# A batched matmul whose engine programs are written by hand, with one counter for every hand-over

## The chip, the cores and the metric

The kernel runs on one core of a Trainium2 chip. The metric is the device time in microseconds (us) from launch to end; before the change the median of 11 runs is 262.08 us (261.91 to 262.48). The profile shows one execution in detail, with the time of each instruction, of each wait and of the DMA traffic.

The engines that matter here are TensorE (PE; its weight loads appear as PEld), VectorE (DVE), ScalarE (ACT) and SyncE (SP). SP does no arithmetic: it issues the transfers between HBM and the on-chip memory. They all go through one queue, which is served by 16 DMA engines.

## The reference

```
x: (16, 768, 512) float32      # batch, k, m
y: (16, 768, 1024) float32     # batch, k, n
out = np.einsum('bkm,bkn->bmn', x, y).astype(np.float32)   # (16, 512, 1024)
```

For each of 16 batches, the product of the transposed x with y. A batch reads 1.57 MB of x and 3.15 MB of y, and writes 2.10 MB.

## The kernel before

A batch is the unit of work. k is split as 128 partitions times KT = 6 slices, m as 128 rows times MT = 4 (`mo`), and n as NT = 2 halves of 512. The stages of a batch are:

1. SP loads x of the batch into a float32 staging tile `xs` (L59) and y into `ys` (L62). There are two buffers of each. The last batch loads y in two halves of three k slices each.
2. VectorE casts `xs` to the bf16 tile `x_sb` in one instruction (L67) and `ys` to `y_sb` in two halves (L70).
3. TensorE runs 48 matmuls of 128x128 by 128x512 (L83): for each of the four `mo`, two halves of n, six k slices added up in PSUM. The last batch does this in two passes, one for each half of k, so that it can start on the first half of y.
4. ScalarE copies each finished `mo` (128x1024, two PSUM banks) into the output tile `o_sb` (L88), four copies for a batch.
5. SP stores `o_sb` (L52). The store of batch b-4 is issued after the loads of batch b; after the loop the last four stores follow. There are five output tiles, and four PSUM buffers of two banks each.

The order of the instructions on each engine is the order in which the program issues them; the tile framework inserts the semaphore waits. On SP this order is: x0 y0, x1 y1, x2 y2, x3 y3, x4 y4 store0, x5 y5 store1, and so on. SP waits in front of a transfer until it may be issued, and everything behind it on SP waits too. The load of x of batch b into its staging buffer waits until the cast of x of batch b-2 has read the buffer; the load of y of batch b waits for both casts of y of batch b-2. Nothing else holds the loads back.

Of the kernel before, what the change touches and what calls it, by code (L numbers as in the profile page):

```python
# [1 line left out]

_os.environ.setdefault("NEURON_RT_ULTRASERVER_MODE", "4")

# [1 line left out]

# [4 lines left out]


@with_exitstack
def kernel(
    ctx: ExitStack,
    tc: tile.TileContext,
    x: bass.AP,
    y: bass.AP,
    out: bass.AP,
):  # L20
    nc = tc.nc
    P = 128
    FP32 = mybir.dt.float32
    BF16 = mybir.dt.bfloat16

    B, K, M = x.shape
    _, _, N = y.shape
    KT = K // P
    MT = M // P
    NF = 512  # L30
    NT = N // NF

    x_v = x.rearrange("b (p ko) m -> b p ko m", ko=KT)
    y_v = y.rearrange("b (p ko) n -> b p ko n", ko=KT)
    o_v = out.rearrange("b (p mo) n -> b p mo n", mo=MT)

    xs_pool = ctx.enter_context(tc.tile_pool(name="xs_pool", bufs=2))
    ys_pool = ctx.enter_context(tc.tile_pool(name="ys_pool", bufs=2))  # L40
    x_pool = ctx.enter_context(tc.tile_pool(name="x_pool", bufs=2))
    y_pool = ctx.enter_context(tc.tile_pool(name="y_pool", bufs=2))
    o_pool = ctx.enter_context(tc.tile_pool(name="o_pool", bufs=5))
    psum = ctx.enter_context(tc.tile_pool(name="psum", bufs=4, space=bass.MemoryType.PSUM))
    LAG = 4
    KH = KT // 2
    o_tiles = {}

    def store(b):
        o_sb = o_tiles.pop(b)  # L50

        nc.sync.dma_start(o_v[b], o_sb[:])  # L52

    with tc.manual_schedule():
        for b in range(B):
            xs = xs_pool.tile([P, KT, M], FP32, name="xs")
            ys = ys_pool.tile([P, KT, N], FP32, name="ys")
            halves = 2 if b == B - 1 else 1
            nc.sync.dma_start(xs[:], x_v[b])  # L59
            for h in range(halves):  # L60
                ks = slice(h * KT // halves, (h + 1) * KT // halves)
                nc.sync.dma_start(ys[:, ks], y_v[b, :, ks])  # L62
            if b >= LAG:
                store(b - LAG)
            x_sb = x_pool.tile([P, KT, M], BF16, name="x_sb")
            y_sb = y_pool.tile([P, KT, N], BF16, name="y_sb")
            nc.vector.tensor_copy(x_sb[:], xs[:])  # L67
            for h in range(2):
                ks = slice(h * KH, (h + 1) * KH)
                nc.vector.tensor_copy(y_sb[:, ks], ys[:, ks])  # L70
            x_w = x_sb[:].rearrange("p k (j mo) -> p k mo j", mo=MT)
            o_sb = o_pool.tile([P, MT, N], FP32, name="o_sb")
            o_tiles[b] = o_sb
            ps = {}


            for h in range(halves):
                for mo in range(MT):
                    if h == 0:
                        ps[mo] = psum.tile([P, NT, NF], FP32, name="ps")  # L80
                    for nt in range(NT):
                        for kt in range(h * KT // halves, (h + 1) * KT // halves):
                            nc.tensor.matmul(  # L83
                                ps[mo][:, nt], x_w[:, kt, mo],
                                y_sb[:, kt, nt * NF:(nt + 1) * NF],
                                start=(kt == 0), stop=(kt == KT - 1))
                    if h == halves - 1:
                        nc.scalar.copy(o_sb[:, mo].rearrange("p (t f) -> p t f", f=NF), ps[mo][:])  # L88
        for b in sorted(o_tiles):
            store(b)  # L90


# [1 line left out]
_INS = ['x', 'y']  # L94
_OUTS = [((16, 512, 1024), 'float32')]


# [23 lines left out]
```

## Time and profile before

| | |
|---|---|
| median of 11 runs | 262.08 us |
| the profiled execution: time, span | 262.1 us, 260.3 us |
| PE busy | 187.5 us, 72% (753 matmuls recorded) |
| DVE busy | 83.1 us, 32% |
| ACT busy | 66.2 us, 25% |
| DMA traffic | 109.18 MB, mean 419 GB/s |
| HBM read, written | 75.50 MB, 33.55 MB |

The span runs from the first to the last instruction; 1.8 us of the profiled execution's time lie outside it. Times inside the profile are counted from the start of the span.

### The profile page before, as it was taken

What the parts mean: (1) busy time and instruction counts of PE and PEld (TensorE: products, weight loads), DVE (VectorE), ACT (ScalarE), POOL (GpSimd) and SP (SyncE); (2) the same over time, 40 slices, a digit from 0 to 9 for tenths busy, and PEclk for the clock granted to TensorE, in tenths of its full rate; (3) what the DMA queues carried; (4) which work ended last, traced back from release to release, by engine and by line L of the source; (5) the groups of instructions that cost most, each with busy time, mean ns of one, the idle gap of its engine ahead of it and who ended that gap; (6) DMA issues with size and microseconds to landing.
All of it is one profiled execution on the core that took longest, in us unless ns stands there. A gap on an engine that the chain in (4) does not pass through costs nothing.

```text
span 260.3 us, 1800 instructions
## 1 busy us (share of the span) xinstructions
PE 187.5 (72%) x753; PEld 88.7 (34%) x768; DVE 83.1 (32%) x48; ACT 66.2 (25%) x65; POOL 0.2 (0%) x4
## 2 busy tenths in 40 slices
PE   0049999898938939599594886939679594899500
PEld 0014555453513514235152342514325152355200
DVE  0271734525223252222524215252132522252000
ACT  1003343333321313313132140412304133131600
POOL 0000000000000000000000000000000000000000
PEclk9999999999997988959799797998979799799965
DMA  7999999999999999999999999999999999999994
GB/s 274 429 427 425 440 429 442 423 389 419 435 427 432 423 436 442 417 437 423 432 438 422 444 409 442 432 424 442 424 437 411 431 442 420 427 431 430 431 431 211
DMA packets 7065, 109.18 MB, mean 419 GB/s; under 512 B 784, under 2 KB 784, under 8 KB 784
## 3 DMA queue, kind: packets, MB, share of 16 engines
q1 hardware_dynamic: 7056, 109.06, 98.4%
q8 instruction: 6, 0.10, 0.1%
q14 instruction: 3, 0.02, 0.0%
HBM read 75.50 MB, written 33.55 MB: 419 GB/s over the span
## 4 chain that ended last, share of the span: by engine, by line
DMA 74%; DVE 11%; PE 8%; ACT 0%; issue 0%; SPq 0%; DVEq 0%
DMA ys<-in_y_dram 74%; DVE y_sb L70 11%; PE ps L83 8%; ACT o_sb L88 0%; SPq L59 0%; DVEq L70 0%
## 5 line engine op out<-in xcount | busy, mean ns | idle before, releaser
L83 PE MATMUL ps<-y_sb,x_sb 128*128 128x512 bf16 x753 | 187.5, 408 | 57.1 <-DVE y_sb L70 56.2
L83 PEld LDWEIGHTS <-x_sb 128*128 128x128 bf16 x768 | 88.7, 117 | 155.4 <-issue 42.5
L88 ACT COPY o_sb<-ps 128x1024 f32<-128x1024 f32 x64 | 64.9, 1014 | 178.8 <-PE ps L83 177.3
L70 DVE CAST y_sb<-ys 128x3072 bf16<-128x3072 f32 x32 | 54.9, 1756 | 88.0 <-DMA ys<-in_y_dram 88.0
L67 DVE CAST x_sb<-xs 128x3072 bf16<-128x3072 f32 x16 | 28.2, 1760 | 65.9 <-DMA xs<-in_x_dram 65.5
L88 ACT ACT_TABLE_LOAD x1 | 1.3, 1283 | 0.7 <-PEq L105 0.7
L105 POOL MEMSET const-bfloat16-1.0<- 128x1 bf16 x1 | 0.1, 103 | 0.0
L105 POOL MEMSET const-uint8-127<- 128x1 uint8 x1 | 0.1, 101 | 0.0
L105 POOL MEMSET const-float32-0.0<- 128x1 f32 x1 | 0.1, 100 | 0.2 <-issue 0.2
L105 POOL MEMSET const-float32-1.0<- 128x1 f32 x1 | 0.1, 99 | 0.0
## 6 DMA issues: line engine op xcount, KB each, us to landing
ys<-in_y_dram SPq DMA_DIRECT2D x15, 3072.0 KB, 28.1
out_dram<-o_sb SPq DMA_DIRECT2D x16, 2048.0 KB, 32.6
xs<-in_x_dram SPq DMA_DIRECT2D x16, 1536.0 KB, 29.7
ys<-in_y_dram SPq DMA_DIRECT2D x2, 1536.0 KB, 26.1
```

Of the source, the lines that this page charges most:

```text
L67: nc.vector.tensor_copy(x_sb[:], xs[:])
L70: nc.vector.tensor_copy(y_sb[:, ks], ys[:, ks])
L83: nc.tensor.matmul(ps[mo][:, nt], x_w[:, kt, mo], y_sb[:, kt, nt * NF:(nt + 1) * NF], start=(kt == 0), stop=(kt == KT - 1))
L88: nc.scalar.copy(o_sb[:, mo].rearrange("p (t f) -> p t f", f=NF), ps[mo][:])
L105: nc = _bacc.Bacc("TRN2", target_bir_lowering=False, num_devices=1)
```

## The change

The tile pools and the waits that they generate are gone. The kernel allocates its buffers itself and writes each engine's program with explicit waits:

- `groups` counts half batches that TensorE has finished (24 matmuls, two `mo`), two for each batch. It is now what most waits look at: SP before loading x of batch b, SP before storing, VectorE before overwriting a bf16 tile, ScalarE before copying.
- The load of x of batch b (b >= 2) waits for `groups >= 2*(b-2)+1`, which is the first half of batch b-2 finished on TensorE. The load of y of batch b has no wait of its own.
- The store of batch b waits for `groups >= 2*(b+2)` (batch b+1 finished on TensorE), the last two for `outs`, which ScalarE raises.
- y of the last batch is loaded in one transfer, and its matmuls are no longer split in two passes.
- TensorE runs a loop of 8 iterations, each of two batches. `ready` (raised by VectorE, once for a cast) and `room` (raised by ScalarE, once for a freed PSUM half) are credits that it waits for and subtracts, in instructions of their own.
- PSUM is two buffers of four banks, and ScalarE copies 128x2048 at a time: 32 copies where there were 64.
- The kernel stands inside a critical section of the tile framework, which puts branches and a hand-over between SP and the other engines at its start and its end.

The casts, the matmuls' shapes, the number of buffers in the on-chip memory and the order of the transfers on SP stay the same.

```diff
-    with tc.manual_schedule():
-        for b in range(B):
...
-            halves = 2 if b == B - 1 else 1
-            nc.sync.dma_start(xs[:], x_v[b])
-            for h in range(halves):
-                ks = slice(h * KT // halves, (h + 1) * KT // halves)
-                nc.sync.dma_start(ys[:, ks], y_v[b, :, ks])
-            if b >= LAG:
-                store(b - LAG)
...
+    ctx.enter_context(tc.tile_critical())
...
+    ps = [ec(nc.psum_tensor(f"ps{i}", [P, HB, NT, NF], FP32)) for i in range(2)]
...
     def store(b):
...
+        if b < B - 2:
+            nc.sync.wait_ge(groups, 2 * (b + 2))
+        else:
+            nc.sync.wait_ge(outs, b - (B - 3))
+        nc.sync.dma_start(o_v[b], ob[b % NO][:]).then_inc(so[b % NO], 16)
+
+    for b in range(B):
+        i = b % 2
+        if b >= 2:
+
+            nc.sync.wait_ge(groups, 2 * (b - 2) + 1)
+        nc.sync.dma_start(xs[i][:], x_v[b]).then_inc(sx[i], 16)
+        nc.sync.dma_start(ys[i][:], y_v[b]).then_inc(sy[i], 16)
+        if b >= LAG:
+            store(b - LAG)
+    for b in range(B - LAG, B):
+        store(b)
+
+
+    for b in range(B):
+        i = b % 2
+        n = 16 * (b // 2 + 1)
+        if b >= 2:
+            nc.vector.wait_ge(groups, 2 * (b - 1))
+        nc.vector.wait_ge(sx[i], n)
+        nc.vector.tensor_copy(xb[i][:], xs[i][:]).then_inc(ready, 1)
+        nc.vector.wait_ge(sy[i], n)
+        for h in range(2):
+            ks = slice(h * KH, (h + 1) * KH)
+            nc.vector.tensor_copy(yb[i][:, ks], ys[i][:, ks]).then_inc(ready, 1)
+
+
+    def batch(i):
+        x_w = xb[i][:].rearrange("p k (j mo) -> p k mo j", mo=MT)
+        nc.tensor.wait_ge(ready, 2).then_inc(ready, -2)
+        for g in range(2):
+            nc.tensor.wait_ge(room, 1).then_inc(room, -1)
+            for m in range(HB):
+                for nt in range(NT):
+                    for kt in range(KT):
+                        if g == 0 and m == 0 and nt == 0 and kt == KH:
+                            nc.tensor.wait_ge(ready, 1).then_inc(ready, -1)
+                        mm = nc.tensor.matmul(
+                            ps[g][:, m, nt], x_w[:, kt, g * HB + m],
+                            yb[i][:, kt, nt * NF:(nt + 1) * NF],
+                            start=(kt == 0), stop=(kt == KT - 1))
+            mm.then_inc(groups, 1)
+
+    pe = nc.tensor.engine
+    with nc.Fori(0, B // 2, engines=OrderedEngineSet([pe]), head_slot={pe: 0}):
+        batch(0)
+        batch(1)
+
+
+    nc.scalar.nop().then_inc(room, 2)
+    for b in range(B):
+        if b >= NO:
+            nc.scalar.wait_ge(so[b % NO], 16 * (b // NO))
+        for g in range(2):
+            nc.scalar.wait_ge(groups, 2 * b + g + 1)
+            cp = nc.scalar.copy(ob[b % NO][:, g * HB:(g + 1) * HB].rearrange("p m (t f) -> p m t f", f=NF),
+                                ps[g][:])
+            if b < B - 1:
+                cp.then_inc(room, 1)
+        if b == B - 2:
+            nc.scalar.drain().then_inc(outs, 1)
+    cp.then_inc(outs, 1)
+
+    for i in range(NO):
+        nc.sync.wait_ge(so[i], 16 * len(range(i, B, NO)))
```

More of the change, by code (lines that the diff above doesn't have):

```diff
@@ L10 @@
 from concourse._compat import with_exitstack
+from concourse.ordered_engine_set import OrderedEngineSet
 @with_exitstack
@@ L37 @@
     o_v = out.rearrange("b (p mo) n -> b p mo n", mo=MT)
[L39 to L44, printed above, removed]
@@ L45 @@
     LAG = 4
+    NO = 5
     KH = KT // 2
-    o_tiles = {}
-    def store(b):
-        o_sb = o_tiles.pop(b)
-        nc.sync.dma_start(o_v[b], o_sb[:])
-    with tc.manual_schedule():
-        for b in range(B):
-            xs = xs_pool.tile([P, KT, M], FP32, name="xs")
-            ys = ys_pool.tile([P, KT, N], FP32, name="ys")
-            halves = 2 if b == B - 1 else 1
-            nc.sync.dma_start(xs[:], x_v[b])
-            for h in range(halves):
-                ks = slice(h * KT // halves, (h + 1) * KT // halves)
-                nc.sync.dma_start(ys[:, ks], y_v[b, :, ks])
-            if b >= LAG:
-                store(b - LAG)
[L65 to L90, printed above, removed]
@@ new lines @@
+    ctx.enter_context(tc.tile_critical())
+    ec = ctx.enter_context
+    xs = [ec(nc.sbuf_tensor(f"xs{i}", [P, KT, M], FP32)) for i in range(2)]
+    ys = [ec(nc.sbuf_tensor(f"ys{i}", [P, KT, N], FP32)) for i in range(2)]
+    xb = [ec(nc.sbuf_tensor(f"xb{i}", [P, KT, M], BF16)) for i in range(2)]
+    yb = [ec(nc.sbuf_tensor(f"yb{i}", [P, KT, N], BF16)) for i in range(2)]
+    ob = [ec(nc.sbuf_tensor(f"ob{i}", [P, MT, N], FP32)) for i in range(NO)]
+    HB = MT // 2
+    ps = [ec(nc.psum_tensor(f"ps{i}", [P, HB, NT, NF], FP32)) for i in range(2)]
@@ new lines @@
+    sx = [ec(nc.semaphore(f"sx{i}")) for i in range(2)]
+    sy = [ec(nc.semaphore(f"sy{i}")) for i in range(2)]
+    so = [ec(nc.semaphore(f"so{i}")) for i in range(NO)]
+    ready = ec(nc.semaphore("ready"))
+    room = ec(nc.semaphore("room"))
+    groups = ec(nc.semaphore("groups"))
+    outs = ec(nc.semaphore("outs"))
+    def store(b):
+        if b < B - 2:
[3 more added lines that the diff above has]
+        nc.sync.dma_start(o_v[b], ob[b % NO][:]).then_inc(so[b % NO], 16)
```

## The prediction

> **What bounds the kernel now.** I read the page's slices and queue table first:
>
> ```profile
> PE   0049999898938939599594886939679594899500
> DMA  7999999999999999999999999999999999999994
> q1 hardware_dynamic: 7056, 109.06, 98.4%
> ```
>
> The DMA digit is 9 in every slice except the first and last, while PE (72% busy), DVE (32%) and ACT (25%) have room. So the transfers are the bound: the end moves when the DMA engines sit idle somewhere, hardly otherwise. The chain of waits gives 74% to the loads of y, which agrees. What matters is how far ahead SP keeps the queue filled. VectorE's timeline gives the landings, since each cast starts when its load has landed:
>
> ```profile
> 7.40 1.76 DVE L67 CAST x_sb<-xs 128x3072 bf16<-128x3072 f32 x1 [7.40 <-DMA xs<-in_x_dram]
> 14.70 3.43 DVE L70 CAST y_sb<-ys 128x3072 bf16<-128x3072 f32 x2 [5.54 <-DMA ys<-in_y_dram]
> 25.70 3.43 DVE L70 CAST y_sb<-ys 128x3072 bf16<-128x3072 f32 x2 [5.55 <-DMA ys<-in_y_dram]
> 36.76 3.43 DVE L70 CAST y_sb<-ys 128x3072 bf16<-128x3072 f32 x2 [5.47 <-DMA ys<-in_y_dram]
> 48.52 3.43 DVE L70 CAST y_sb<-ys 128x3072 bf16<-128x3072 f32 x2 [5.53 <-DMA ys<-in_y_dram]
> ```
>
> One batch of loads (4.72 MB) takes 25.70 - 14.70 = 11.0 us, 429 GB/s. By bytes, x is 3.67 us, y 7.33, a store 4.88. SP's timeline shows the issues:
>
> ```profile
> 0.73 0.38 SPq L59 DMA_DIRECT2D xs<-in_x_dram  x1
> 9.19 0.33 SPq L59 DMA_DIRECT2D xs<-in_x_dram  x1
> 18.15 0.33 SPq L62 DMA_DIRECT2D ys<-in_y_dram  x1
> 20.18 0.33 SPq L59 DMA_DIRECT2D xs<-in_x_dram  x1
> ```
>
> x0, issued at 0.73 into an empty queue, is used at 7.40: 6.67 us, of which 3.0 are not its own bytes. x2 is issued at 9.19, 16.5 us before y1 ahead of it has landed, so today this 3.0 is hidden. ScalarE's timeline tells when TensorE finishes each `mo`:
>
> ```profile
> 21.76 1.01 ACT L88 COPY o_sb<-ps 128x1024 f32<-128x1024 f32 x1 [19.75 <-PE ps L83]
> 24.35 1.01 ACT L88 COPY o_sb<-ps 128x1024 f32<-128x1024 f32 x1 [1.58 <-PE ps L83]
> 34.71 1.01 ACT L88 COPY o_sb<-ps 128x1024 f32<-128x1024 f32 x1 [1.58 <-PE ps L83]
> ```
>
> 24.35 and 34.71 are the second `mo` of batches 0 and 1: what the new counter calls the first half finished. A warm `mo` (12 matmuls) takes 2.59 us, 0.216 a matmul.
>
> [...] Here the nine matmuls before 21.76 (from 18.18) took 0.40 us each, later ones 0.216[...].
>
> **The change, part by part.**
>
> *The wait before x loads.* Until now x2 waited for the cast of x0 (issue at 9.19). Now it waits for the first half of batch 0 on TensorE, 24.35, so issue at 24.4; y2, x3 and all later transfers stand behind it on SP. Into an empty queue it is used at 24.4 + 6.67 = 31.07; behind y1 without a gap it would have been 25.70 + 3.67 = 29.37. The queue runs dry: **1.7 us** lost, and as it is full from then to the end, no later stage gives this back. Bounds: had TensorE been warm from 18.18, the half would end at 18.18 + 21 x 0.216 = 22.7, loss 0.1; warm only 2 us later than here, about 1.0 more, 2.7.
>
> x3 waits for batch 1's first half, 34.71. Empty queue: 34.75 + 6.67 = 41.4; behind y2 (now 36.7 + 1.7 = 38.4): 42.1. No gap, slack 0.7. x4: y2 at 38.4, casts 3.44, then 21 matmuls 4.53: issue 46.4, 53.1 from an empty queue; y3 lands 11.76 after y2 (48.52 - 36.76), so 50.2 + 3.67 = 53.8. Slack 0.7; with y3 after 11.0, none. I take 0 (0 to 0.3). From x5 on a store stands in the queue too, slack 5 us; in the steady state x(b+2) is issued 9.7 us after y(b) (219.46 to the second `mo` at 229.13), while 24.4 us of transfers stand between their landings, against 9.7 + 6.7. Nothing lost.
>
> *The last batch.* Before, at the tail, by the whole timeline:
>
> ```profile
> 222.94 21.70 PE L83 MATMUL ps<-y_sb,x_sb 128*128 128x512 bf16 x91 [0.82 <-DVE y_sb L70]
> 235.27 1.76 DVE L70 CAST y_sb<-ys 128x3072 bf16<-128x3072 f32 x1 [1.83 <-DMA ys<-in_y_dram]
> 244.67 1.01 ACT L88 COPY o_sb<-ps 128x1024 f32<-128x1024 f32 x1 [0.28 <-PE ps L83]
> ```
>
> y15's second half lands at 235.25; the last store lands 13.7 us after its issue at 245.7, at 259.4, which is 24.2 after y15: five stores of 4.88. So 10.5 us of compute after y15 are covered. Undivided, y15 needs two casts 3.44, then 45 matmuls (batch 14: 222.9 to 234.31, 11.4, with a partly cold clock; 9.7 warm), then a copy of 128x2048 (not in the trace; twice 1.01 = 2.02 above, 1.01 below): 16.95. The store alone takes 3.0 + 4.88, so it lands at 24.8 against 24.2: 0.6 lost; warm, nothing. I take **0.3** (0 to 0.7). Stores 12 to 14 are ready earlier (batch 14 ends before y15 has landed).
>
> *TensorE's credit instructions and loop.* Three waits a batch now stand alone, so weights are loaded only behind them (one load is 117 ns): **0.2** (0 to 0.4) on x2's issue, elsewhere covered by slack. The back edge:[...] nothing here shows one. Batches 0 and 1 cross none before x2 and x3, batch 2 does: inside the slack.
>
> *ScalarE's larger copies, PSUM in two halves, VectorE's waits:* TensorE finds the other half free, since a copy of some 2 us ends within the 5.18 us of the next half. Uncovered they would delay TensorE by 2 us at most, which stops loads only where the slack above is under 1.
>
> *Start and end.* Two more branches ahead of the first load[...]: **0.1**. At the end one more hand-over between SP and the engines; the last waits of SP show two such, 0.6 us in all (L116 <- PEq), so **0.3** (0 to 0.6). Fewer TensorE instructions to fetch: the instruction queue moved 0.10 MB, at 429 GB/s 0.2 us: **-0.1** (-0.2 to 0).
>
> Sum: 1.7 + 0 + 0.3 + 0.2 + 0.1 + 0.3 - 0.1 = 2.5. On the profiled execution's 262.1 (span 260.3, 1.8 around it) that makes 264.6; it stands at the median of 262.08, so 264.6, +0.95%.
>
> **Rivals.**
>
> *The gap does not open.* If x2's data start sooner than x0's did (the first packets show about 0.8 us after its issue, though the rate is full only at 3 us) and TensorE is warm early, the loss at x2 is near 0 and the tail is warm: 262.1 + 0.4 = 262.5, within the noise. Against it: cold start of TensorE is what the trace shows. 0.10.
>
> *Faster.* The 1.8 us outside the span might hold the fetch of the long unrolled program. If most of it, say 1.5 us, goes, and the gap at x2 is under 0.5, the time is about 262.1 - 1.5 + 0.5 + 0.3 = 261.4. It decides where the saving exceeds gap plus exit by 0.5. For it: TensorE's rows shrink from 1536 to a loop body of some 100. Against it: no row shows a wait for instructions at the start. 0.06.
>
> *TensorE's back edge stalls.* [...] At the price of a DMA in an empty queue, 3.0 us, batch 2 is late by 3.0, x4 by 3.0 less its slack of 0.7: 264.6 + 2.3 = 266.9; later batches have 5 us or more. Against it: the body is short. It decides when the stall is over 0.7. No trace shows it. 0.10.
>
> **How the numbers follow.** The forecast has 0.74, its own range 263.2 to 265.8 (the x2 gap 0.1 to 2.7, less its ends). The overall range starts at 262.5, taking in the first rival, and goes to 266.2, short of the third: about 0.2 left out. A change within 0.2% (0.52 us) is about what a measurement cannot tell from none. Slower: 0.74 + 0.10 = 0.84; same 0.10; faster 0.06.
>
> **What would show it.** Right: the DMA digit falls in the slice at 19.5 to 26 us or the one after it, x2 issued near 24.4, its cast near 31.1, y2 at 38.4, later intervals as before; the last store issued near 254, close to when the queue runs out. Wrong: DMA at full rate through 24 to 27 us; or a second gap near 47 us (the loop), or a tail gap over 1 us (TensorE cold, or copies slower than 2.02 us). A different time outside the span would speak for the faster case.

## The result, and the profile after

The changed kernel takes 266.14 us (median of 8 runs, 265.39 to 267.4) against 262.16 us for the kernel before (30 runs): a ratio of 1.0153, 95% interval 1.0142 to 1.0164. The profiled execution and one more run, of 267.43, are not in this median; with them it is 266.20. It is slower by 3.98 us where 2.5 was forecast: above the forecast's own range (263.2 to 265.8), and only just inside the overall range, which ends at 266.2. Run again later in another group (6 runs), it took 266.84 us, ratio 1.0182 (1.0158 to 1.0206), so its own groups of runs differ by 0.7 us.

The profiled execution of the changed kernel took 267.18 us, with a span of 265.2, and is one of its slower ones; that of the kernel before took 262.1, with 260.3. From the page of the changed kernel, the slices and the queue:

```profile
PE   0029998987874959769397783948969396895930
DMA  7996999999999999999999999999999999999984
q1 hardware_dynamic: 6912, 109.05, 97.1%
```

The fourth DMA digit has fallen from 9 to 6: that is the slice from 19.9 to 26.5 us. No later digit falls below 9 until the end, where the last two are 8 and 4 (before: 9 and 4). VectorE's timeline, with the landings (start of each cast, its duration, engine and line):

```profile
8.76 1.76 DVE L92 CAST xb<-xs 128x3072 bf16<-128x3072 f32 x1 [8.76 <-DMA xs<-in_x_dram]
16.06 3.43 DVE L96 CAST yb<-ys 128x3072 bf16<-128x3072 f32 x2 [5.54 <-DMA ys<-in_y_dram]
27.04 3.43 DVE L96 CAST yb<-ys 128x3072 bf16<-128x3072 f32 x2 [5.53 <-DMA ys<-in_y_dram]
32.51 1.76 DVE L92 CAST xb<-xs 128x3072 bf16<-128x3072 f32 x1 [2.04 <-DMA xs<-in_x_dram]
39.73 3.43 DVE L96 CAST yb<-ys 128x3072 bf16<-128x3072 f32 x2 [5.46 <-DMA ys<-in_y_dram]
51.42 3.43 DVE L96 CAST yb<-ys 128x3072 bf16<-128x3072 f32 x2 [5.46 <-DMA ys<-in_y_dram]
```

y2 comes 2.97 us later than before (39.73 against 36.76). But y0 and y1 were already 1.36 and 1.34 late, ahead of any changed wait on the loads. SP's timeline and ScalarE's timeline:

```profile
0.94 0.38 SPq L78 DMA_DIRECT2D xs<-in_x_dram  x1
26.08 0.33 SPq L78 DMA_DIRECT2D xs<-in_x_dram  x1
36.44 0.33 SPq L78 DMA_DIRECT2D xs<-in_x_dram  x1
48.03 0.33 SPq L78 DMA_DIRECT2D xs<-in_x_dram  x1
```

```profile
26.09 1.87 ACT L127 COPY ob<-ps 128x2048 f32<-128x2048 f32 x1 [23.84 <-PE ps L109]
36.45 1.87 ACT L127 COPY ob<-ps 128x2048 f32<-128x2048 f32 x1 [3.31 <-PE ps L109]
254.05 1.87 ACT L127 COPY ob<-ps 128x2048 f32<-128x2048 f32 x1 [3.25 <-PE ps L109]
```

x2 and x3 are issued at the moment when ScalarE may copy the first half of batches 0 and 1 (26.08 and 26.09, 36.44 and 36.45): the new wait decides both. A copy of 128x2048 takes 1.87 us. The stretches from 22 to 30 us (columns: the stretch, its length, busy time of PE, PEld, DVE, ACT and POOL with the number of instructions in brackets, PE's clock, DMA share, GB/s):

```profile
22.00:24.00 2.00, 2.00 (x8) 0.83 (x7) 0.00 (x0) 0.00 (x0) 0.00 (x0) 1.00 1.00 430
24.00:26.00 2.00, 2.00 (x11) 1.08 (x10) 0.00 (x0) 0.00 (x0) 0.00 (x0) 1.00 0.20 86
26.00:28.00 2.00, 2.00 (x11) 1.02 (x10) 0.96 (x1) 1.87 (x1) 0.00 (x0) 1.00 0.54 98
28.00:30.00 2.00, 2.00 (x11) 1.03 (x10) 2.00 (x2) 0.00 (x0) 0.00 (x0) 1.00 0.83 356
```

TensorE is busy throughout, while the transfers drop to 86 and 98 GB/s for four microseconds: the queue has run dry.

A load counts as landed when the last of the 16 DMA engines has delivered its part (x0 in the changed kernel: the ninth engine at 6.92 us, the last at 8.73, the cast at 8.76). The trace holds 16 landings for each transfer, one for each engine, and they differ. The table gives the ninth of them, called the median engine, and the last, in the profiled executions (read from the 16 semaphore events of each transfer). All rows but the first two are kernels of the experiments below:

```
us, median engine / last engine
                              x2           x3           x4           y4            y15
before                   28.77/29.36  39.88/41.11  50.88/52.11  58.68/60.32  232.96/235.25
changed                  32.16/32.41  43.55/44.11  54.60/55.55  62.55/64.22  236.95/239.71
all loads freed (e1)     28.96/30.82  39.96/41.82  50.95/52.80  58.80/61.19  232.84/235.36
x2 freed (e2)            28.96/31.14  42.28/44.94  53.61/56.13  61.93/64.32  235.96/238.33
x2, x3 freed (e6)        28.92/31.15  39.91/42.15  53.68/54.02  62.18/62.36  236.40/238.39
x2, x3, x4 freed (e7)    28.91/31.12  39.91/42.11  50.92/53.11  58.72/61.68  233.02/235.69
TensorE kept warm (e5)   29.45/30.92  41.68/42.42  53.10/54.32  61.15/63.04  235.36/237.89
x2 later (e3)            37.37/37.96  48.35/48.96  60.53/61.16  69.01/69.70  243.27/245.21
loop written out (e9)    30.14/30.45  41.67/42.61  53.47/56.15  61.57/64.61  235.65/238.71
changed again (e12)      32.63/32.88  43.92/44.50  54.90/55.80  63.01/64.44  237.05/239.32
```

### The profile page after: what moved, and what is told of

It reads as the page before. It is cut to its first block, busy times and chain, and to the rows that moved or that the text cites. A ratio compares the mean times of both kernels' runs of the same rounds, so it can differ in the third digit from the quotient of the medians.

```text
span 265.2 us, 1823 instructions
## 1 busy us (share of the span) xinstructions
PE 187.7 (71%) x760; PEld 87.0 (33%) x768; DVE 83.0 (31%) x48; ACT 61.1 (23%) x33; POOL 0.2 (0%) x4
## 5 line engine op out<-in xcount | busy, mean ns | idle before, releaser
L109 PE MATMUL ps<-yb,xb 128*128 128x512 bf16 x760 | 187.7, 406 | 66.4 <-PEq L103 58.5
L109 PEld LDWEIGHTS ps<-yb,xb 128*128 128x128 bf16 x768 | 87.0, 116 | 166.5 <-issue 101.5
L127 ACT COPY ob<-ps 128x2048 f32<-128x2048 f32 x32 | 59.8, 1869 | 193.9 <-PE ps L109 193.9
L96 DVE CAST yb<-ys 128x3072 bf16<-128x3072 f32 x32 | 54.8, 1756 | 90.2 <-DMA ys<-in_y_dram 90.2
L92 DVE CAST xb<-xs 128x3072 bf16<-128x3072 f32 x16 | 28.2, 1760 | 69.9 <-DMA xs<-in_x_dram 69.9
```

What stands on the lines that cost most here:

```text
L92: nc.vector.tensor_copy(xb[i][:], xs[i][:]).then_inc(ready, 1)
L96: nc.vector.tensor_copy(yb[i][:, ks], ys[i][:, ks]).then_inc(ready, 1)
L109: mm = nc.tensor.matmul(ps[g][:, m, nt], x_w[:, kt, g * HB + m], yb[i][:, kt, nt * NF:(nt + 1) * NF], start=(kt == 0), stop=(kt == KT - 1))
L127: cp = nc.scalar.copy(ob[b % NO][:, g * HB:(g + 1) * HB].rearrange("p m (t f) -> p m t f", f=NF), ps[g][:])
```

## The experiments

Theory A: the waits on TensorE at the first loads leave the queue dry, and this sets the time. Theory B: the loads are in time anyway, and the time goes to hand-overs, the loop and the tail.

### All loads released by the casts (e1)

Two counters, `cx` and `cy`, are raised by VectorE behind its cast of x and its second cast of y. All else is the changed kernel.

```diff
-            nc.sync.wait_ge(groups, 2 * (b - 2) + 1)
+            nc.sync.wait_ge(cx, b - 1)
         nc.sync.dma_start(xs[i][:], x_v[b]).then_inc(sx[i], 16)
+        if b >= 2:
+            nc.sync.wait_ge(cy, b - 1)
         nc.sync.dma_start(ys[i][:], y_v[b]).then_inc(sy[i], 16)
...
         nc.vector.tensor_copy(xb[i][:], xs[i][:]).then_inc(ready, 1)
+        nc.vector.drain().then_inc(cx, 1)
...
```

> x and y of batch b are loaded as before the change, behind the casts of batch b-2; all else is as in the changed kernel. Theory A (the queue runs dry because x2 waits for TensorE's first half of batch 0): x2 is issued near 10.5 us, no empty stretch in the DMA rate at 24 to 27 us, time 263.5 us (262.9 to 264.4), since the late start of one DMA engine, the exit and the time outside the span stay. Theory B (the loads are in time anyway and the time goes to hand-overs, the loop and the tail): 265.5 us or more.

Measured: 262.92 us (20 runs), ratio 1.003 (1.0023 to 1.0037). The same stretches:

```profile
22.00:24.00 2.00, 2.00 (x10) 0.94 (x8) 0.00 (x0) 0.00 (x0) 0.00 (x0) 1.00 1.05 455
24.00:26.00 2.00, 2.00 (x11) 1.02 (x9) 0.00 (x0) 0.21 (x1) 0.00 (x0) 1.00 0.88 375
26.00:28.00 2.00, 2.00 (x11) 1.05 (x10) 0.84 (x1) 1.66 (x1) 0.00 (x0) 1.00 1.04 442
28.00:30.00 2.00, 2.00 (x11) 1.07 (x10) 2.00 (x2) 0.00 (x0) 0.00 (x0) 1.00 1.05 449
```

The hole is gone, and 3.22 of the 3.98 us with it (266.14 - 262.92; by the later group's median it would be 3.9). The loop, the credits, PSUM in two halves and the wide copies are all still in this kernel, so with the loads in time they cost, together with the longer start and end, 0.76. Theory B falls.

### Which of the loads matters (e2, e6, e7)

Only the loads of the batches named are released by the casts, the rest wait for TensorE. For e2 (e6 has `b < 4` and e7 `b < 5`, and the same bound for y):

```diff
-            nc.sync.wait_ge(groups, 2 * (b - 2) + 1)
+            if b == 2:
+                nc.sync.wait_ge(cx, 1)
+            else:
+                nc.sync.wait_ge(groups, 2 * (b - 2) + 1)
...
```

> Only the loads of batch 2 are released by the casts; from batch 3 on the loads wait for TensorE as in the changed kernel. Theory A with my prediction's claim that only x2 loses: within 0.8 us above the kernel that frees all loads (a gap of 0.4 to 1.1 us may open at x3, which is issued near 36.4 us). If the later waits cost as much as the first, it is 1.5 us or more above it. Theory B: as the changed kernel, 266.1 us.

Measured: 265.12 us (4 runs), ratio 1.01 (1.0083 to 1.0117), 2.2 us above the kernel that frees all loads. The claim that x2 alone matters fell. In SP's timeline of this kernel the loads of x2, y2 and x3; and from VectorE's, the casts of y2 and x3:

```profile
11.00 0.33 SPq L83 DMA_DIRECT2D xs<-in_x_dram  x1
19.99 0.33 SPq L86 DMA_DIRECT2D ys<-in_y_dram  x1
36.34 0.33 SPq L83 DMA_DIRECT2D xs<-in_x_dram  x1
```

```profile
38.44 3.43 DVE L104 CAST yb<-ys 128x3072 bf16<-128x3072 f32 x2 [5.44 <-DMA ys<-in_y_dram]
45.03 1.76 DVE L99 CAST xb<-xs 128x3072 bf16<-128x3072 f32 x1 [3.16 <-DMA xs<-in_x_dram]
```

x2 is now in time, and the hole sits at x3 instead: x3 follows y2 after 6.6 us, where its bytes need 3.67. Hence the next kernel, and a model to go with it. Between 18.6 and 51.8 us TensorE runs without a stop in each of the four kernels that free x2 by its cast (e1, e2, e6, e7). In the one that frees all loads its first halves end at 25.79, 36.15 and 46.51 us, 10.36 apart, while the loads of a batch take 11.0. So in this model each load that waits for TensorE is late, each a little less than the one before, and the largest delay that is left is what is paid.

> The loads of batches 2 and 3 are released by the casts, those from batch 4 on by TensorE. Pacing model (TensorE is late by 16 us at the start and catches up on the queue by 0.6 us a batch: x2 3.4 us late, x3 2.8, x4 2.2, x5 not at all since a store stands in the queue; the largest lateness that is left is what is paid): 2.2 us or a little less above the kernel that frees all loads, 264.5 to 265.2. Sum model (each wait pays for itself, x3 and later almost nothing): at most 0.5 above it, 262.9 to 263.4.

Measured: 265.58 us (4 runs), ratio 1.0129 (1.0112 to 1.0146), 2.7 above the kernel that frees all loads. The sum model falls. In the table, x4 is 2.73 us late on the median engine (53.68 against 50.95). That is more than the 2.2 of the model, and the time is above the 264.5 to 265.2 written down; TensorE's first half ended at 26.97 here, against 25.98 in e2, and x4 was issued at 47.68, against 46.75.

> The loads of batches 2, 3 and 4 are released by the casts, those from batch 5 on by TensorE. Pacing model: nothing is left, 262.9 us (262.6 to 263.3). If the waits cost something in the steady state too, more than 263.5.

Measured: 262.86 us (5 runs), ratio 1.0038 (1.0023 to 1.0052), as much as with all loads freed. So the waits of x2, x3 and x4 carry all that freeing the loads wins, and from batch 5 on the wait for TensorE costs nothing. The losses do not add up: behind the hole that the first late load makes, the later ones add little (the rows of the changed kernel and of e1: 3.20 us at x2, 3.65 at x4).

### A later x2 (e3)

```diff
-            nc.sync.wait_ge(groups, 2 * (b - 2) + 1)
+            nc.sync.wait_ge(groups, 2 if b == 2 else 2 * (b - 2) + 1)
```

> Only the load of x of batch 2 waits longer: for the second half of batch 0 on TensorE, 5.2 us after the first. Theory A: all of it is lost, 266.1 + 5.2 = 271.3 us, and the empty stretch at 24 to 27 us grows by 5.2 us. Theory B: under 268 us.

Measured: 272.93 us (2 runs), ratio 1.04 (1.0377 to 1.0423); 6.8 or 6.1 us above the two medians of the changed kernel, more than the 5.2 expected, on few runs. The profiled executions compare more closely: x2 is issued at 31.44 in place of 26.08, 5.36 later, and the time is 272.74 against 267.18, 5.56 more. So a delay at the first hole comes back at the end, as theory A has it, and here a little more than all of it. The table shows where the rest may come from: against the changed kernel the median engine is 5.21 us later at x2 but 5.93 at x4, which waits for TensorE in its turn and was issued only at 54.42.

### TensorE warm before batch 0 (e4, e5)

In the changed kernel the matmuls of batch 0 begin 0.38 to 0.43 us apart up to 23.0 us, but for one wait, and from 23.3 us on 0.216 apart (called warm here). Extra matmuls on x0, written over later, run ahead of the loop, to see whether batch 0 then starts at the faster pace:

```diff
+    nc.tensor.wait_ge(ready, 1)
+    for k in range(18):     # 26 in e5
+        nc.tensor.matmul(ps[0][:, 0, 0], xb[0][:, 0, 0:P], xb[0][:, k % KT], start=True, stop=True)
     pe = nc.tensor.engine
```

> 18 matmuls whose results are written over run on TensorE between the cast of x0 and the first real matmul[...]; all else is as in the changed kernel. Theory A: the first half of batch 0 ends near 24.0 us in place of 26.1, x2 is issued as much earlier, and the time falls by about that, to 264.1 us (263.6 to 265.0). Theory B: no change, 266.1 us.

Measured: 266.68 us (4 runs, 265.38 to 268.9), ratio 1.0161 (1.0093 to 1.0229): no gain. TensorE's timeline shows the warm-up end too early:

```profile
9.47 5.99 PE L117 MATMUL ps<-xb 128*128 128x512 bf16 x18 [9.47 <-DVE xb L92]
18.28 0.81 PE L109 MATMUL ps<-yb,xb 128*128 128x512 bf16 x3 [2.82 <-PEq L103]
```

TensorE was idle for 2.82 us, the granted clock was at half from 20.2 to 23.7 us by its record (0.56 from 20 to 22, 0.59 from 22 to 24), and x2 was issued at 26.21. The experiment did not do what it was made for, so it says nothing on either theory.

> As the warm-up before, with 26 matmuls in place of 18, so that TensorE is not idle between the warm-up and batch 0 (with 18 it idled from 15.5 to 18.3 us, and its clock fell back to half at 20.2). Theory A: the first half of batch 0 ends near 24.0 us, x2 is issued then, and the time falls by 1 to 2 us to 264.1 to 265.1; if the warm-up runs past the cast of y0 it gives part of that back. If the issue time of x2 does not set the time: 266.1.

Measured: 264.63 us (4 runs), ratio 1.0095 (1.0078 to 1.0111). TensorE's timeline:

```profile
9.56 7.58 PE L117 MATMUL ps<-xb 128*128 128x512 bf16 x26 [9.56 <-DVE xb L92]
17.10 0.81 PE L109 MATMUL ps<-yb,xb 128*128 128x512 bf16 x3
18.62 9.88 PE L109 MATMUL ps<-yb,xb 128*128 128x512 bf16 x45 [0.71 <-PEq L108]
```

x2 is issued at 23.35, 2.7 us earlier than in the changed kernel, and the time falls by 1.5 (266.14 - 264.63). But the faster pace of batch 0 (45 matmuls in 9.88 us, 0.22 each) is not the only difference. From the first matmul of batch 0 to the issue of x2 it takes 6.25 us (23.35 - 17.10) in place of 7.96 (26.08 - 18.12), 1.7 less; the other 1.0 is an earlier start, because the last engine delivered y0 at 15.02 in place of 16.04. The extra matmuls had moved a fetch of instructions, from 4.11 to 16.65 us (more on it at e8). So an earlier issue of x2 gains time, and TensorE's slow start (0.43 us a matmul in place of 0.22) makes up 1.7 us of the issue time; what it costs by itself at the end is not separated. Less than 2.7 comes back because x3, issued at 35.59, and x4, issued at 46.72, are late in their turn: 1.7 and 2.15 us on the median engine (41.68 against 39.96, 53.10 against 50.95).

### The loop written out (e8, e9)

```diff
-    pe = nc.tensor.engine
-    with nc.Fori(0, B // 2, engines=OrderedEngineSet([pe]), head_slot={pe: 0}):
-        batch(0)
-        batch(1)
+    for b in range(B):
+        batch(b % 2)
```

e8 does this in the kernel with all loads freed, e9 in the changed kernel.

> As the kernel that frees all loads, and TensorE's program is written out for 16 batches in place of the loop. If the loop costs nothing: 262.9 (262.6 to 263.2). If the fetch of its block at 4.1 us, which holds one DMA engine for 0.93 us, is what makes the first landings 1.4 us late, x0 lands at 7.5 in place of 8.8 us and the time falls by up to 0.5, unless the later fetches of the longer program give it back. If the back edge stalls TensorE, its gaps between pairs of batches shrink but the time stays.

Measured: 262.75 us (8 runs), ratio 1.003 (1.0019 to 1.0041), the ratio of the kernel with the loop. x0 is used at 7.71 in place of 8.86. In the changed kernel one packet of 16 KB on the instruction queue at 4.11 us took 0.93 us; with the program written out there is none before 37 us. Over all traces this goes together: in the eight that have such a fetch between 4.1 and 4.6 us the last engine delivers x0 at 8.7 to 9.2 us, in the other six at 7.1 to 7.7. So that fetch does make the last engine late at the start; it does not show in the time while the queue stays full. Neither would a stall of the loop where it jumps back, since TensorE has time to spare here. TensorE's timeline of the changed kernel shows the first jump itself, between batches 1 and 2:

```profile
18.12 23.47 PE L109 MATMUL ps<-yb,xb 128*128 128x512 bf16 x95 [18.12 <-PEq L103]
41.79 0.81 PE L109 MATMUL ps<-yb,xb 128*128 128x512 bf16 x3 [0.20 <-PEq L103]
```

Batch 1 ends at 41.59 and batch 2 begins 0.20 us later, 0.30 behind the cast that it needs (39.73 + 1.76), just as batch 0 begins 0.30 behind its own (16.06 + 1.76). The jump takes no time of its own that can be seen.

> The changed kernel with its waits as they are, and TensorE's program written out in place of the loop. If the fetch of the loop's block (16 KB at 4.1 us, one DMA engine held for 0.93 us) makes the landings of x0 and y0 late and through them TensorE's start: x0 is used near 7.7 us in place of 8.8, x2 issued near 25.0 in place of 26.1, and the time falls by about 1.1, to 265.0 us (264.6 to 265.6). If the loop has no part in it: 266.1.

Measured: 266.75 us (4 runs), ratio 1.0186 (1.017 to 1.0201): not the 265.0 expected. x0 is used at 7.21 and x2 issued at 24.22, so the earlier start is there, but x4 is issued at 47.40, only 0.6 us earlier than in the changed kernel (48.03). The profiled execution (266.20) is 1.0 below that of the changed kernel, the median is not.

> The changed kernel again, unaltered, for the scatter of its time and a second trace. If the program written out is really slower than the loop by 0.6 us: 266.1 (265.9 to 266.4). If the difference is scatter between groups of runs, this median may lie anywhere from 265.4 to 267.2. In the trace the median DMA engine should again land x2 3.2 us later than in the kernel that frees the loads (32.2 against 29.0 us).

Measured: 266.84 us (6 runs, 266.09 to 268.19), x2 on the median engine at 32.63. Against this median the written-out program (266.75) is neither better nor worse. The loop costs nothing that these runs can tell; whether the earlier first landings gain something with the waits in place stays open.

The table shows why an earlier x2 may gain little. The time goes roughly with the delay that is left at x4, not with that at x2. Against the kernel that frees all loads (whose profiled execution took 262.84), on the median engine:

```
                            delay at x2   delay at x4   longer by, us
TensorE kept warm (e5)          0.49          2.15          2.45
loop written out (e9)           1.18          2.52          3.36
x2 freed (e2)                   0.00          2.66          2.95
x2, x3 freed (e6)              -0.04          2.73          2.92
changed                         3.20          3.65          4.34
changed again (e12)             3.67          3.95          3.98
```

These are single executions, so it is an observation that agrees with the model of e6, not a further proof of it.

### The tail (e10)

The kernel with all loads freed, and y15 in two halves on semaphores of their own, each cast behind its half.

```diff
-        nc.sync.dma_start(ys[i][:], y_v[b]).then_inc(sy[i], 16)
+        if b < B - 1:
+            nc.sync.dma_start(ys[i][:], y_v[b]).then_inc(sy[i], 16)
+        else:
+            nc.sync.dma_start(ys[i][:, :KH], y_v[b, :, :KH]).then_inc(sl[0], 16)
+            nc.sync.dma_start(ys[i][:, KH:], y_v[b, :, KH:]).then_inc(sl[1], 16)
...
```

> All loads freed by the casts, and y of the last batch loaded in two halves, each cast behind its own half; TensorE still runs its matmuls in the order of the loop. My prediction's step (an undivided y15 costs 0 to 0.7 us at the tail): 262.6, up to 0.3 less than the kernel that only frees the loads. What its trace says (the last store follows the one before it after 4.86 us on the slowest DMA engine, so that engine never waits): no change, 262.9 (262.7 to 263.1).

Measured: 263.18 us (5 runs), ratio 1.0045 (1.0032 to 1.0059): no gain. TensorE's two passes over the last batch are not restored here, but the last store is issued at 249.44 in place of 251.70, 2.3 us earlier, and nothing comes of it. So the undivided y15 costs nothing at the tail.

### The hand-over at the end (e11)

The kernel before, with an empty critical section behind it:

```diff
         for b in sorted(o_tiles):
             store(b)
+    with tc.tile_critical():
+        nc.sync.nop()
```

> The kernel before the change with an empty critical section behind its last store, which adds the hand-over between SP and the other engines at the end. If the hand-over is what makes the end of the changed kernel longer by 0.3 us in the span: 262.4 to 262.7, and 1.1 to 1.2 us from the last landing to the end of the span in place of 0.9. If not: 262.1.

Measured: 263.14 us (5 runs), ratio 1.0044 (1.0031 to 1.0058), 1.1 us more. From the last landing (259.52) to the end of the span (261.2) it takes 1.7 us in place of 0.9. So such a section does cost time at the end; 1.1 us where at most 0.6 was expected, and more than in the changed kernel, where the same stretch is 1.2 us (263.96 to 265.2). In e11 SP has many more semaphores to wait for in front of the hand-over (twelve by its trace), which may be why; that was not tried.

## Why the prediction was right or wrong

*Right: the bound, the mechanism, the sign.* The transfers are the bound, the wait on TensorE in front of the first x loads empties the queue, and nothing gives the time back. Freeing those loads takes 3.22 of 3.98 us away; freeing x2 to x4 alone does the same. That the time still fell inside the overall range is partly luck: it is above the range of the forecast's own sum, and the second group's median, 266.84, lies outside both.

*The size of the gap at x2 was too small: 1.7, with 0.2 for the credits, where the loads cost 3.2.* Two steps were wrong.

- *The issue time.* Worked out as 24.4, with the credits and the start 24.7; it was 26.08. The start is 0.21 later (0.94 against 0.73). The last engine delivered x0 and y0 another 1.15 later, because the block of the loop was fetched at 4.11 us (e8); the prediction booked the fetches as a gain of 0.1. And the first matmul starts 0.30 us after its cast ends (16.06 + 1.76 to 18.12) where it was 0.05 (14.70 + 1.76 to 16.51, TensorE's first line before): that 0.25 is what the credits cost, near the 0.2 taken.

```profile
16.51 1.44 PE L83 MATMUL ps<-y_sb,x_sb 128*128 128x512 bf16 x3 [16.51 <-DVE y_sb L70]
```

- *Where the queue runs dry.* The step added the bytes of x2 to the landing of y1, 25.70, which is the landing on the last engine. With the changed kernel's own times it gives 26.08 + 6.67 - (27.04 + 3.67) = 2.0, so the issue time alone does not make up the 3.2: most engines had run dry before the last one landed y1 (the median engine had it at 25.18, the last at 27.02). In the kernel with all loads freed the median engine has x2 at 28.96 and the last at 30.82; in the changed kernel they are at 32.16 and 32.41. The hole makes all engines start afresh together, so the last loses 1.6 and the median 3.2. What is lost in the end is the larger: by y15 the last engine is 4.35 later than in the kernel with all loads freed (239.71 against 235.36), the median 4.11. These two executions are 4.34 apart, more than their medians; that the 3.2 at x2 equals the 3.22 of the medians is in part chance (in e12 it is 3.67). In both of them the last engine falls behind the median again, to 2.8 and 2.5 us, whatever the hole had evened out. Why it lags is not settled: the second trace of the changed kernel has a last engine only 0.2 us behind the next.

The latency of 3.0 us out of an empty queue held: x2 was used 6.43 us after its issue (26.08 to 32.51), against 6.67 for x0 before. The bounds of the gap at x2, 0.1 and 2.7, rest on when TensorE's matmuls quicken, which was the author's estimate: it was 21.1 us in the trace before and 23.0 in the changed kernel, 4.6 and 4.9 us after the first matmul.

*x3 and x4: no gap expected behind the gap of x2.* Nearly so: on the median engine the delay against the freed kernel goes from 3.2 at x2 to 3.6 at x3 and 3.65 at x4. What I made of it before the second experiment, that the wait on x3 is harmless, was wrong: it is harmless only because x2 is late.

*Steady state: nothing lost.* Right (e7).

*The last batch: 0.3.* It costs nothing (e10). (The prediction's sum of 16.95 is 16.86 from its own terms, which does not change the 0.3.) In the changed kernel the last store lands 4.83 us after the one before on the last engine (259.13 to 263.96), its own 4.88: this engine never waits. The median engine does (251.68 to 262.11 for two stores, 10.4 in place of 9.7), but it is not the one that ends last. The wide copy takes 1.87 us, near the 2.02 taken. The partly cold clock named there for batch 14 is a granted clock of 0.63 from 222 to 224 us and 0.52 from 224 to 226.

*Start and end: 0.1, 0.3 and -0.1 for the fetches.* The 0.1 for two branches was the author's estimate, which no trace had shown. Measured with the loads freed: start 0.21, last landing to the end of the span 0.3 longer, and the time outside the span 1.96 us against 1.77 (medians of the runs), 0.19 more; 0.7 in all where 0.3 was taken, next to the 0.76 that this kernel is slower. The 0.19 outside the span is unexplained. So the gap was taken 1.3 too small and these three 0.4, and the 0.3 for the last batch, which was not needed, hid a part of that.

*The rivals.* The gap opened, so the first falls. The faster case looked for a saving outside the span; that part grew. A stall where the loop jumps back falls with TensorE's timeline at 41.59 to 41.79 us, shown at e8; no trace had shown such a stall, and its 3.0 us was an estimate from x0's landing.

## What to carry to other kernels

Where the transfers are the bound, ask of a counter that many waits share whether it moves a load's release to a later engine. By the prediction's estimate, which e7 bears out from batch 5 on, that is harmless where the queue holds more work than that engine's delay plus the restart of an empty queue (3.0 us by x0 before, 2.8 by x2 in the changed kernel, 6.43 - 3.67). Look at the first batches: here no stores stood in the queue, TensorE's first matmuls came 0.43 us apart in place of 0.22, it was still catching up (10.36 us a batch against 11.0 for the loads), and three of the fourteen waits cost 1.2%. And freeing the first late load alone may gain little, because the next one is late too.

## What the runs showed of the hardware

- The 16 DMA engines drift apart under one queue: the last one lands a load up to 3.1 us after the median (238.71 against 235.65 for y15 in e9), and behind a hole in the queue they are close together again (0.25 us apart at x2 in the changed kernel, 0.34 at x4 in e6).
- One fetch of 16 KB of instructions took 0.9 to 1.1 us as one packet. Where it fell at 4.1 to 4.6 us, the last engine delivered x0 at 8.7 to 9.2 us in place of 7.1 to 7.7.
- With the waits in instructions of their own, TensorE's first matmul began 0.30 us after the end of the cast that it needs; in the kernel before it was 0.05.
- TensorE's first matmuls began 0.38 to 0.43 us apart, but for one wait, up to 21.1 us in the kernel before and 23.0 in the changed kernel, and 0.216 apart from 21.3 and 23.3 on; behind 26 extra matmuls (e5) the 45 from 18.62 us took 9.88, 0.22 each.
- Of the four pauses of TensorE of 2.7 to 2.9 us in the changed kernel, three of 2.7 (from 96.03, 191.60 and 239.04) went with a granted clock of half from 98.24, 193.82 and 241.60, while one of 2.87 (from 144.02) had none; in e4, with a pause of 2.82, it came 2 us after the matmuls had begun again.
